# A layer's second expert product: unsplit weight chunks replaced by split ones, with some low parts made on GpSimd

## The chip, the cores and the metric

The kernel runs on one core of one Trainium2 chip. A core has TensorE (PE in the profile; PEld is its weight load), VectorE (DVE), ScalarE (ACT), GpSimd (POOL), SyncE (SP) and 16 DMA engines. The metric is the device time of one execution in microseconds. The kernel before takes 967.09 us (median of three runs, 965.84 to 968.64).

## The reference

One decoder layer on 256 tokens of width 1024. A mixer (a retention branch and a block attention branch, gated and merged) is added to the residual stream. Then comes the part that matters here, a product-key lookup among 16384 single-neuron experts:

```python
def peer(h, w_q, sub_keys, u_tab, v_tab):
    ...
    experts = jnp.take_along_axis(cand_i, pos, axis=-1)      # 16 experts for each of 8 heads, per token
    gates = jax.nn.softmax(top_s, axis=-1).astype(h.dtype)
    ...
        u = u_tab[ec]
        a = jax.nn.gelu(jnp.einsum('td,thkd->thk', hc, u), approximate=False)
        return jnp.einsum('thk,thkd->td', gc * a, v_tab[ec])
```

Both tables are 16384 x 1024 in 32-bit floats (64 MB each). The result is 256 x 1024, in 32-bit floats.

## The kernel before

The kernel first computes the mixer and the queries. For most tokens it then reads the experts densely: the first expert product multiplies the whole table u, in 128 chunks of 128 experts, with the tokens, and the result, after its activation and gates, is the matrix W (128 experts x 128 chunks x 176 token columns). For the remaining tokens it gathers rows: GpSimd issues an indirect DMA for each (line 1026, tiles `rows`), and VectorE adds the row, scaled, to a running sum (line 1112, tiles `vacc` and `accx`).

The second expert product is the loop at the end: for every chunk c of the table v, 8 blocks of 128 columns are multiplied with the chunk's 176 columns of W. Eight PSUM banks `o` add up over all chunks.

A chunk of v arrives by one 512 KB DMA on SP's queue, into one of the six slots of `raw_ring`. There are two ways to multiply it:

- Split. ScalarE copies the chunk to `rhi` in the format fp32r (line 148, the high part), and VectorE subtracts that from the chunk and writes `rlo` (line 149, the low part). This is `split_to`, called by `cut_v`. `cut_w` does the same with W for two chunks at once: `cw` holds the high part (ScalarE, line 1234) and the low part (VectorE, line 1235) side by side. A block is then two matmuls: high part of v with 352 columns (line 1294), and low part of v with 176 columns (line 1295).
- Unsplit. For the ten pairs of chunks that `PLAIN` lists, TensorE multiplies the raw chunk with W in 32-bit floats (line 1292), and neither ScalarE nor VectorE touches them.

`rhi` and `rlo` have four buffers each, taken in turn in the order of the calls, and `cw` has two. The schedule is written by hand: instructions stand on each engine's queue in the order of the calls, each queue runs in order, and semaphores between the engines follow from the tiles that they read and write. In iteration c the program asks for chunk c+2's cut, multiplies chunk c, and takes 0.62 steps of the gather.

## Time and profile before

| | |
|---|---|
| median of the runs | 967.09 us |
| the profiled execution | 966.36 us, its span 964.6 us |
| TensorE busy | 956.3 us (99%) |
| VectorE busy | 770.8 us (80%) |
| ScalarE busy | 518.9 us (54%) |
| GpSimd busy | 362.8 us (38%) |
| moved by DMA | 318.30 MB, 330 GB/s on the mean |

The second expert product begins 672.35 us into the span. Rows of a timeline give the start, the duration, the engine, the line, the operation with what it writes and reads, and in brackets the idle time of the engine just before it with what ended it. Rows of stretches give, for each engine, the busy time and the instructions in it, then TensorE's granted share of its clock, the share of the DMA engines and the rate. In the chain of waits, a row gives the start, the duration, the engine, the tile and the line.

### The profile page before, as it was taken

The numbers are of one execution on the slowest core, as the hardware profiler recorded it, in microseconds if no ns is written. First come the engines' busy times: TensorE is split into PE (matmuls) and PEld (weight loads), VectorE is DVE, ScalarE is ACT, GpSimd is POOL, SyncE is SP. The second block draws the span as 40 slices with busy tenths as digits, with TensorE's granted clock in tenths as the row PEclk, the third lists the DMA queues.
The fourth block names the chain that finished last, engine by engine and source line by source line (L and its number), as shares of the span: only waits on it lengthen the run. The fifth ranks groups of instructions, "written<-read, shape, count | busy, mean of one in ns | idle before, by whom it ended". The sixth has DMA issues, their size and how long they took to land.

```text
span 964.6 us, 19141 instructions
## 1 busy us (share of the span) xinstructions
PE 956.3 (99%) x7216; PEld 917.8 (95%) x7216; DVE 770.8 (80%) x1487; ACT 518.9 (54%) x946; POOL 362.8 (38%) x303
## 2 busy tenths in 40 slices
PE   8999999999999999999999999999999999999998
PEld 6887898998999999999999999999999999999997
DVE  6667667777679997999689998844888888988886
ACT  5555555544654445444667776975454444544443
POOL 2421000000204456444455676744444553554520
PEclk9999999999999999999999999999999999999999
DMA  8877889996798999999999999999999999999993
GB/s 297 243 186 228 241 240 270 305 290 187 243 395 330 407 369 344 380 374 389 370 377 336 367 335 371 384 327 365 331 386 388 390 392 365 386 387 385 380 349 111
DMA packets 108042, 318.30 MB, mean 330 GB/s; under 512 B 11276, under 2 KB 21397, under 8 KB 107822
## 3 DMA queue, kind: packets, MB, share of 16 engines
q1 hardware_dynamic: 64524, 184.43, 53.6%
q0 software_dynamic: 32528, 115.54, 32.2%
q10 hardware_dynamic: 10898, 17.11, 5.9%
q8 instruction: 57, 0.93, 0.4%
q14 instruction: 35, 0.29, 0.1%
HBM read 306.47 MB, written 12.09 MB: 330 GB/s over the span
## 4 chain that ended last, share of the span: by engine, by line
PE 96%; DMA 2%; DVE 1%; issue 0%; ACT 0%; POOL 0%; SPq 0%; ACTq 0%; DVEq 0%; POOLq 0%
PE acc L1262 23%; PE side L736 10%; PE acc L1294 8%; PE side L1294 8%; PE acc L231 6%; PE acc L233 6%; PE acc L232 6%; PE acc L1190 4%; PE acc L1295 4%; PE side L1295 4%; PE acc L241 3%; PE acc L240 3%; PE acc L242 3%; PE side L1292 3%; PE acc L1292 2%; DMA raw_ring<-in_peer_u_dram 2%
## 5 line engine op out<-in xcount | busy, mean ns | idle before, releaser
L1026 POOL DMA_INDIRECT rows<-in_peer_u_dram,eg x86 | 108.2, 1259 | 78.5 <-DVE rows L1037 34.6
L1026 POOL DMA_INDIRECT rows<-in_peer_v_dram,eg x54 | 86.9, 1610 | 90.2 <-DVE vacc L1112 66.7
L736 PE MATMUL side<-ident,raw_ring 128*128 128x128 f32 x816 | 107.2, 274 | 0.8 <-DMA raw_ring<-in_peer_u_dram 0.8
L736 PEld LDWEIGHTS side<-ident,raw_ring 128*128 128x128 f32 x816 | 98.7, 190 | 1.2 <-issue 1.2
L1037 DVE SCALAR_TENSOR_TENSOR rows<-rows,h 128x1024 f32<-128x1024 f32 x43 | 53.2, 1247 | 5.5 <-DMA rows<-in_peer_u_dram,eg 5.3
L1112 DVE SCALAR_TENSOR_TENSOR vacc<-rows,av,vacc 128x1024 f32<-128x1024 f32 x43 | 55.0, 1280 | 0.2
L1205 ACT ACTIVATE W<-acc 128x512 f32<-128x512 f32 (+17 forms) x44 | 28.0, 636 | 32.2 <-DVE W L1203 25.9
L1220 POOL TENSOR_TENSOR W<-W,gl 128x256 f32<-128x256 f32 (+16 forms) x29 | 25.0, 861 | 52.6 <-ACT gl L1219 45.7
L1234 ACT ACTIVATE cw<-W 128x352 fp32r<-128x352 f32 x54 | 26.6, 492 | 31.9 <-PE acc L1295 29.6
L1235 DVE TENSOR_TENSOR cw<-W,cw 128x352 fp32r<-128x352 f32 x54 | 28.1, 521 | 18.2 <-ACT cw L1234 17.8
L1150 DVE TENSOR_TENSOR oh_buf<-niota,tT 128x512 f32<-128x512 f32 x44 | 32.5, 738 | 6.6 <-ACT tT L1172 6.6
L579 POOL DMA_DIRECT2D x1d<-xt x1 | 0.7, 657 | 88.2 <-DVE xt L561 88.2
L155 POOL TENSOR_TENSOR gny<-va,minus_half 128x8 f32<-128x8 f32 x2 | 3.3, 1654 | 69.6 <-DVE va L453 69.6
L1156 ACT ACTIVATE oh_buf<-oh_more,tT 128x128 f32<-128x128 bf16 x88 | 29.4, 425 | 0.1
L1156 ACT ACTIVATE oh_more<-oh_more,tT 128x128 f32<-128x128 bf16 x88 | 29.2, 423 | 0.0
L1203 DVE TENSOR_TENSOR W<-acc,W 128x280 f32<-128x280 f32 (+16 forms) x32 | 24.7, 770 | 5.5 <-PE acc L1190 2.8
L1292 PE MATMUL side<-W,raw_ring 128*128 128x176 f32 x160 | 27.4, 314 | 0.0
L1262 PE MATMUL acc<-hTd,raw_ring 128*128 128x128 f32 x224 | 27.3, 275 | 0.0
L1292 PE MATMUL acc<-W,raw_ring 128*128 128x176 f32 x160 | 27.1, 313 | 0.0
L1262 PEld LDWEIGHTS acc<-hTd,raw_ring 128*128 128x128 f32 x224 | 26.1, 192 | 0.0
L1292 PEld LDWEIGHTS acc<-W,raw_ring 128*128 128x128 f32 x160 | 24.7, 190 | 0.0
L1292 PEld LDWEIGHTS side<-W,raw_ring 128*128 128x128 f32 x160 | 24.3, 190 | 0.0
(2623 smaller groups left out, 3446.2 us busy)
## 6 DMA issues: line engine op xcount, KB each, us to landing
raw_ring<-in_peer_v_dram SPq DMA_DIRECT2D x128, 512.0 KB
raw_ring<-in_peer_u_dram SPq DMA_DIRECT2D x102, 512.0 KB
raw_ring<-in_w_in_dram SPq DMA_DIRECT2D x52, 512.0 KB
raw_ring<-in_peer_w_q_dram SPq DMA_DIRECT2D x16, 512.0 KB
raw_ring<-turned SPq DMA_DIRECT2D x14, 512.0 KB
W<-in_peer_u_dram SPq DMA_DIRECT2D x12, 512.0 KB
raw_ring<-in_ret_w_branch_dram SPq DMA_DIRECT2D x8, 512.0 KB
raw_ring<-in_w_out_dram SPq DMA_DIRECT2D x8, 512.0 KB
```

Source lines behind the costliest of these rows:

```text
L231: T.matmul(o[t], xh[:, s], wh, start=(k == 0), stop=False)
L232: T.matmul(o[t], xh[:, s], wl, start=False, stop=False)
L233: T.matmul(o[t], xl[:, s], wh, start=False, stop=(k == kc - 1))
L736: T.transpose(p[:, k * P:(k + 1) * P], r.rearrange("p (i k) -> p k i", k=KC)[:, 4 * q + k], ident)
L1026: G.indirect_dma_start(out=r, out_offset=None, in_=tab, in_offset=bass.IndirectOffsetOnAxis(ap=eg[:, j:j + 1], axis=0))
L1037: V.scalar_tensor_tensor(r, r, 1.0, h, op0=OP.mult, op1=OP.mult, accum_out=av[:, j:j + 1])
L1112: V.scalar_tensor_tensor(a, r, av[:, j:j + 1], a, op0=OP.mult, op1=OP.add)
L1156: A.activation(o1[:, j], o1b[:, :, j], AF.Copy, scale=tT[:, t, 1, k + j:k + j + 1])
L1262: T.matmul(pa[:, n:n + NA], uT[:, k * P:(k + 1) * P], hT[:, k], start=(c % 2 == 0 and k == 0), stop=(k == KC - 1), skip_group_check=True)
L1292: T.matmul(o[b][:, :ND], vh[:, n], w, start=False, stop=False, skip_group_check=True)
L1294: T.matmul(o[b][:, :2 * ND], vh[:, n], w, start=(c == 0), stop=False, skip_group_check=True)
L1295: T.matmul(o[b][:, :ND], vl[:, n], w[:, :ND], start=False, stop=(c == NK - 1), skip_group_check=True)
```

## The change

All chunks are split, so `PLAIN` and the unsplit branch are gone. Every sixth chunk from 9 on (`LOW_G`: 9, 15, ... 123, twenty chunks) has its low part made by GpSimd, and its cut is asked for in iteration c-3, ahead of the cut of the chunk before it. All others are cut two ahead as before.

```diff
-PLAIN = [4 + 6 * i for i in range(10)]
+LOW_G = range(9, 125, 6)
...
     def cut_v(c):
         if c < NK:
             hi, lo = hi_tile(), lo_tile()
-            split_to(hi, lo, v_raw.pop(c))
+            split_to(hi, lo, v_raw.pop(c), G if c in LOW_G else V)
             v_cut[c] = (hi, lo)
...
     def block(b, c):
         vh, vl, w = cuts[c]
         n = slice(b * P, (b + 1) * P)
-        if vl is None:
-            T.matmul(o[b][:, :ND], vh[:, n], w, start=False, stop=False, skip_group_check=True)
-            return
         T.matmul(o[b][:, :2 * ND], vh[:, n], w, start=(c == 0), stop=False, skip_group_check=True)
         T.matmul(o[b][:, :ND], vl[:, n], w[:, :ND], start=False, stop=(c == NK - 1), skip_group_check=True)
...
     for c in range(NK):
         load_to(len(pieces) + NK + c + 2)
-        if (c + 2) // 2 not in PLAIN:
+        if c + 3 in LOW_G:
+            cut_v(c + 3)
+        if c + 2 not in LOW_G:
             cut_v(c + 2)
-            if c % 2 == 0:
-                cut_w(c + 2)
-        if c // 2 in PLAIN:
-            cuts[c] = (v_raw.pop(c), None, W[:, c, :])
-        else:
-            cuts[c] = (*v_cut.pop(c), w_cut[c - c % 2][:, c % 2])
+        if c % 2 == 0:
+            cut_w(c + 2)
+        cuts[c] = (*v_cut.pop(c), w_cut[c - c % 2][:, c % 2])
```

How the queues change is shown at three places. The first is ScalarE's queue before, around the unsplit chunks 8 and 9 (`rhi__7439` is chunk 7's high part, `rhi__7500` chunk 10's):

```order
L1234 ACTIVATE cw<-W 128x2x176
L148 ACTIVATE rhi__7439<-raw_ring 128x1024
L148 ACTIVATE rhi__7500<-raw_ring 128x1024
L1234 ACTIVATE cw<-W 128x2x176
L148 ACTIVATE rhi__7515<-raw_ring 128x1024
```

and the same place after the change (`rhi__7460` is chunk 9's high part, `rhi__7464` chunk 8's, `rhi__7510` chunk 10's):

```order
+L148 ACTIVATE rhi__7460<-raw_ring 128x1024
+L148 ACTIVATE rhi__7464<-raw_ring 128x1024
+L1234 ACTIVATE cw<-W 128x2x176
+L148 ACTIVATE rhi__7510<-raw_ring 128x1024
+L1234 ACTIVATE cw<-W 128x2x176
+L148 ACTIVATE rhi__7533<-raw_ring 128x1024
```

Chunks 8 and 9 now have high parts and a `cw` of their own, and chunk 9's high part stands ahead of chunk 8's.

The second is VectorE's queue after the change, from chunk 7's low part (`rlo__7440`) over chunk 8's (`rlo__7465`) to chunk 11's (`rlo__7534`):

```order
L149 TENSOR_TENSOR rlo__7440<-raw_ring,rhi__7439 128x1024
L149 TENSOR_TENSOR rlo__7465<-raw_ring,rhi__7464 128x1024
L1235 TENSOR_TENSOR cw<-W,cw 128x2x176
L1112 SCALAR_TENSOR_TENSOR accx<-rows__7172,av,accx 128x1024
L1112 SCALAR_TENSOR_TENSOR accx<-rows__7175,av,accx 128x1024
L149 TENSOR_TENSOR rlo__7511<-raw_ring,rhi__7510 128x1024
L1235 TENSOR_TENSOR cw<-W,cw 128x2x176
L149 TENSOR_TENSOR rlo__7534<-raw_ring,rhi__7533 128x1024
```

Before, chunk 10's low part followed on chunk 7's with only the two gathered rows between. Now chunk 8's low part and its `cw` stand there too; chunk 9's low part isn't on this queue.

The third is GpSimd's queue, before:

```order
L1220 TENSOR_TENSOR W<-W,gl 128x2x128 x4
L1026 DMA rows<-in_peer_v_dram,eg 128x1024 x4
L1026 DMA rows__7496<-in_peer_v_dram,eg 128x1024
L1026 DMA rows__7527<-in_peer_v_dram,eg 128x1024
L1026 DMA rows<-in_peer_v_dram,eg 128x1024 x4
```

and after:

```order
L1220 TENSOR_TENSOR W<-W,gl 128x2x128 x4
L1026 DMA rows<-in_peer_v_dram,eg 128x1024 x3
L149 TENSOR_TENSOR rlo__7461<-raw_ring,rhi__7460 128x1024
L1026 DMA rows<-in_peer_v_dram,eg 128x1024
L1026 DMA rows__7506<-in_peer_v_dram,eg 128x1024
L1026 DMA rows__7553<-in_peer_v_dram,eg 128x1024
L1026 DMA rows<-in_peer_v_dram,eg 128x1024
L149 TENSOR_TENSOR rlo__7605<-raw_ring,rhi__7604 128x1024
```

The gathers are the same ones; after every three to five of them stands the low part of a chunk, here of chunks 9 and 15.

## The prediction

> **What bounds the kernel now.** I read the page's busy table and chain first, then the stretches of the second expert product.

> ```profile
> span 964.6 us, 19141 instructions
> PE 956.3 (99%) x7216; PEld 917.8 (95%) x7216; DVE 770.8 (80%) x1487; ACT 518.9 (54%) x946; POOL 362.8 (38%) x303
> PE 96%; DMA 2%; DVE 1%; issue 0%; ACT 0%; POOL 0%; SPq 0%; ACTq 0%; DVEq 0%; POOLq 0%
> ```

> TensorE is the chain almost from end to end, so time is won by less work on it or lost by a new wait in front of it. The unsplit pairs begin at 690.0, 716.6, 743.2 and so on. Cutting there gives periods of twelve chunks: one unsplit pair and five split pairs.

> ```profile
> core 0: us, PE busy (x) PEld busy (x) DVE busy (x) ACT busy (x) POOL busy (x), PEclk, DMA share, GB/s
> 716.60:743.20 26.60, 26.60 (x194) 26.60 (x194) 22.54 (x23) 12.77 (x15) 10.70 (x7) 1.00 1.00 385
> ...
> 902.70:929.30 26.60, 26.60 (x194) 26.60 (x194) 23.55 (x23) 12.56 (x16) 10.44 (x8) 1.00 1.00 377
> sum 239.30, PE 239.30 PEld 239.30 DVE 205.26 ACT 114.35 POOL 111.35; mean PE 26.59 PEld 26.59 DVE 22.81 ACT 12.71 POOL 12.37
> ```

> Nine periods take 239.3 us, 26.59 each, and TensorE is never idle in them. VectorE works 205.26 / 9 = 22.81 us a period: 3.78 us to spare. ScalarE and GpSimd have half their time free; the DMA engines have almost none.

> **TensorE's gain.** These are the first matmuls of two split chunks eight apart, and two rows of the chain where unsplit pairs begin:

> ```profile
> 723.38 0.35 PE L1294 MATMUL side<-cw,rhi__7778 128*128 128x352 f32 x1
> 740.82 0.36 PE L1294 MATMUL side<-cw,rhi__7961 128*128 128x352 f32 x1
> 716.59 1.22 PE side L1292 x8
> 743.16 1.22 PE side L1292 x8
> ```

> A split chunk takes (740.82 - 723.38) / 8 = 2.18 us, so twelve take 26.16. The old period is 743.16 - 716.59 = 26.57, or 26.59 by the mean of nine. Each of ten periods gains 0.43 us: **-4.3 us** if everything else keeps up.

> **What VectorE must do.** Its work back to back, in one place:

> ```profile
> 718.79 1.22 DVE L149 TENSOR_TENSOR rlo__7779<-raw_ring,rhi__7778 128x1024 fp32r<-128x1024 f32 x1
> 719.93 1.22 DVE L149 TENSOR_TENSOR rlo__7792<-raw_ring,rhi__7791 128x1024 fp32r<-128x1024 f32 x1
> 721.06 0.52 DVE L1235 TENSOR_TENSOR cw<-W,cw 128x352 fp32r<-128x352 f32 x1
> 721.50 1.28 DVE L1112 SCALAR_TENSOR_TENSOR vacc<-rows,av,vacc 128x1024 f32<-128x1024 f32 x1
> 722.69 1.22 DVE L149 TENSOR_TENSOR rlo__7818<-raw_ring,rhi__7817 128x1024 fp32r<-128x1024 f32 x1
> ```

> From start to start, a low part costs 1.14 us, a low part of the weights (`cw`) 0.44, a gathered row's sum 1.19. A period after the change has twelve low parts, of which GpSimd makes two, so VectorE still makes ten. It gets a sixth `cw`: 22.81 + 0.44 = 23.25 us. By that count alone it fits into 26.16.

> **The price of the twenty low parts on GpSimd.** No subtraction of 1024 columns runs there now. The nearest rows are sums and products of two operands; the last VectorE row is the one that they meet.

> ```profile
> 643.99 0.72 POOL L1220 TENSOR_TENSOR W<-W,gl 128x256 f32<-128x256 f32 x1 [3.80 <-ACT gl L1219]
> 66.23 1.28 POOL L325 TENSOR_TENSOR ra<-ra,rb__607 128x512 f32<-128x512 f32 x1 [21.44 <-DVE rb__607 L323]
> 67.48 2.27 POOL L325 TENSOR_TENSOR ra<-ra,rb__613 128x512 f32<-128x512 f32 x1
> 67.36 1.23 DVE L149 TENSOR_TENSOR rlo__624<-raw_ring,rhi__623 128x1024 fp32r<-128x1024 f32 x1
> 68.52 2.32 DVE L149 TENSOR_TENSOR rlo__657<-raw_ring,rhi__656 128x1024 fp32r<-128x1024 f32 x1
> ```

> Undisturbed, 256 columns take 0.72 us and 512 take 1.28; by that slope 1024 take 2.40, an estimate. GpSimd has 14 us free in a period, so two of these fit.

> But the two engines shut each other out. GpSimd's second sum begins at 67.48, just after VectorE began a subtraction (67.36 to 68.59), and lasts 2.27 us: it ends 1.28 after VectorE is through, its whole undisturbed time. VectorE's next subtraction, of the same kind as those in question, begins at 68.52 and takes 2.32 instead of 1.23: it ends 1.08 after GpSimd has ended at 69.75. VectorE lost 1.09 us to 512 columns. A shorter pair agrees:

> ```profile
> 669.64 1.49 POOL L1220 TENSOR_TENSOR W<-W,gl 128x256 f32<-128x256 f32 x1 [3.27 <-ACT gl L1219]
> 669.33 1.22 DVE L149 TENSOR_TENSOR rlo__7279<-raw_ring,rhi__7278 128x1024 fp32r<-128x1024 f32 x1 [0.42 <-ACT rhi__7278 L148]
> 670.55 1.68 DVE L149 TENSOR_TENSOR rlo__7296<-raw_ring,rhi__7295 128x1024 fp32r<-128x1024 f32 x1
> ```

> Here 256 columns cost VectorE 0.46 us and GpSimd 0.77. The same slope takes VectorE's loss to 1.09 + 1.12 = 2.21 us for 1024 columns. All three kinds of VectorE work in this stage read two operands from SBUF, as the delayed subtractions do, so I let all of them be shut out. The bounds are 0 (GpSimd always in a gap of VectorE) and 2.40 (its whole time). I take 2.21, nearest to the same operation's row. The low part taken off VectorE saves 1.14 and costs it 2.21.

> [...] With the whole 2.40 locked a period would be 28.05 instead of 27.67 us and the end result 3.8 us later.

> **The sum.** VectorE's period becomes 23.25 + 2 x 2.21 = 27.67 us, more than TensorE's 26.16 and more than the old 26.59. It becomes the bound and TensorE waits for low parts. Ten periods (chunks 6 to 126) add 10 x (27.67 - 26.59) = 10.8; TensorE's gain is already in this, since it waits.

> VectorE enters with a head start that is used up first. Its first low part ends at 669.33 + 1.22 = 670.55, and TensorE wants that chunk here:

> ```profile
> 672.35 0.41 PE L1294 MATMUL side<-cw,rhi__7278 128*128 128x352 f32 x1
> ```

> That is -1.8 us. Of VectorE's 3.78 us of idleness a period nearly nothing should remain, since its waits are on high parts that are then ready. All of it remaining would be +37.8, none is 0. I take about +1 in all, towards none because a late VectorE finds its inputs waiting. So 10.8 - 1.8 + 1 = **+10.0**.

> **Parts that I cost at nothing.** Twenty more high parts (1.06 us) and ten `cw` copies (0.49) are 2.6 us a period on ScalarE, which has 13.9 free there. The bytes loaded are the same; a raw slot comes free when its low part is made, and no longer after TensorE has read it. At 27.67 us a period the DMA engines need 385 x 26.6 / 27.67 = 370 GB/s. If VectorE did not bind they would need 391, and the split stretch of another period showed 398. GpSimd's gathers queue behind each new subtraction, by up to 2.4 plus 1.2 us of waiting for VectorE. Six rows are in flight and a sum comes every 2.18 / 0.62 = 3.5 us, so about 17 us of lead covers it; without that cover VectorE would wait up to 3.6 us at each of twenty places.

> ```profile
> 827.70:849.50 21.80, 21.80 (x163) 21.80 (x161) 19.08 (x19) 9.60 (x11) 12.99 (x7) 1.00 1.02 398
> 724.03 1.06 ACT L148 ACTIVATE rhi__7838<-raw_ring 128x1024 fp32r<-128x1024 f32 x1 [2.29 <-DMA raw_ring<-in_peer_v_dram]
> 729.92 0.35 PE L1294 MATMUL side<-cw,rhi__7838 128*128 128x352 f32 x1
> ```

> The profiled execution took 966.36 us for its span of 964.6. It becomes 976.4, and the median of the runs shown (967.09) is 0.73 above it: **977 us**.

> **Rivals.**

> *TensorE keeps the pace.* If a GpSimd low part costs VectorE at most (26.16 - 23.25) / 2 = 1.45 us, the ten gains come whole: 967.1 - 4.3 = 962.8. For it: GpSimd starts once ScalarE has written chunk c+3, and ScalarE then spends 1.06 us on chunk c+2, for which VectorE may be idle anyway, so part of the lock could fall into that gap. Against it: with 27.67 us asked of 26.16 there are no gaps left. Chance 0.17.

> *A draw.* At a loss of (26.59 - 23.25) / 2 = 1.67 us the period is the old one, and between 1.6 and 1.8 the time stays within 0.3% (about what a measurement here can tell from no change), at 964 to 970. A larger head start would also lead here. Chance 0.10.

> *ScalarE's new order holds up the chunk ahead.* ScalarE takes chunk c+3 before c+2 at twenty places, and c+3 lands later. In the rows last shown a chunk landed at about 724.0 and was wanted at 729.92, 5.9 us later; the one in front of it 2.18 earlier, 3.7 us after the landing. From the landing of c+3 the new order needs 1.06 (its high part), 2.21 (GpSimd, over the other high part), 1.14 and 0.44: 4.85 us. That is 1.1 late. At half of the places it adds 11 us to the forecast (988), at all 22 (999). It decides once loads land less than 7.0 us ahead of their use. Against it: the ring refills faster without raw chunks held by TensorE, and a slower TensorE lets loads get ahead. Chance 0.13.

> *The forecast*, VectorE bound at 970 to 985: 0.60.

> **Numbers.** The likeliest case gives 977, its own range 970 to 985. Taking in the first rival and the lower half of the third, the range is 962.5 to 989. Faster 0.17, same 0.10, slower 0.73.

> **What would show it.** GpSimd's L149 rows should last 2.4 to 3.6 us, and VectorE rows next to them should grow by about 2.2. VectorE should be busy some 98% between 700 and 930, and TensorE should show idle time ahead of L1294 or L1295 put down to VectorE's `rlo` or `cw`, twenty times 0.7 us on average, with periods of 27.7 us. If TensorE shows no idle time and periods of 26.2, the price of the lock is wrong. If TensorE waits for ScalarE's `rhi`, or ScalarE for DMA at the new places, the third rival holds.

## The result and the profile after

The changed kernel takes 977.47 us (median of six runs, 975.16 to 979.01); the kernel before takes 968.05 beside it (965.84 to 968.64). The ratio is 1.0098, with a 95% interval from 1.0084 to 1.0113: 9.4 us slower. The profiled execution took 977.47 us itself, with a span of 975.7.

The busy table and the shares of the chain, from the page of the changed kernel:

```profile
span 975.7 us, 19251 instructions
PE 957.6 (98%) x7216; PEld 916.8 (94%) x7216; DVE 803.5 (82%) x1497; ACT 543.1 (56%) x976; POOL 431.2 (44%) x323
PE 94%; issue 2%; DVE 2%; POOL 1%; ACT 0%; DMA 0%; ACTq 0%; DVEq 0%; POOLq 0%
```

TensorE's share of the chain falls from 96% to 94%, VectorE's rises from 1% to 2% and GpSimd's from 0% to 1%. How long the stage lasts is read from two rows of its timeline, the first matmul of chunk 0 and that of chunk 126. Line 1291 is now the high part's matmul, line 1292 the low part's (1294 and 1295 before). The third row is the kernel before, its first matmul of chunk 126.

```profile
671.00 0.41 PE L1291 MATMUL side<-cw,rhi__7278 128*128 128x352 f32 x1
964.17 0.35 PE L1291 MATMUL side<-cw,rhi__10277 128*128 128x352 f32 x1
953.07 0.35 PE L1294 MATMUL side<-cw,rhi__10017 128*128 128x352 f32 x1
```

That is 293.2 us for 126 chunks. Before it was 953.07 - 672.35 = 280.7. The stage is 12.4 us longer; the part ahead of it ended 1.35 us earlier in this execution. Against 126 x 2.18 = 274.7 us the excess is 18.5: 12.4 of it are chunks late by over 0.2 us after a wait, 3.4 are two stretches at half clock (below), 1.7 are the small matmuls of the gathered sum near chunk 124, which every version has, and 1.0 is in smaller delays. Before, the excess was 6.0: the same 1.7 and 4.3 for the unsplit pairs.

The waits of TensorE in this stage (what it waited for; us in total, times, longest):

```profile
PE side L1291 <- DVE cw L1235: 7.5, 9, 2.6
PE side L1292 <- DVE rlo__10018 L149: 1.9, 1, 1.9
PE side L1292 <- POOL rlo__8752 L149: 1.1, 1, 1.1
```

The waits sum to 10.5 us. A chunk is late by up to 0.2 us more than its wait, which makes up the rest of the 12.4. TensorE had none of these waits before. Its releaser is VectorE ten times out of eleven, and nine of them name `cw`. Two of the nine periods of twelve chunks, and the sum of all nine:

```profile
core 0: us, PE busy (x) PEld busy (x) DVE busy (x) ACT busy (x) POOL busy (x), PEclk, DMA share, GB/s
711.20:737.30 26.10, 26.10 (x194) 26.10 (x193) 24.02 (x24) 16.00 (x19) 20.05 (x11) 1.00 1.01 384
820.40:851.30 30.90, 28.18 (x194) 27.76 (x193) 26.53 (x24) 15.07 (x19) 18.69 (x11) 0.94 0.96 375
sum 248.30, PE 239.75 PEld 237.40 DVE 233.75 ACT 136.12 POOL 175.74; mean PE 26.64 PEld 26.38 DVE 25.97 ACT 15.12 POOL 19.53
```

The mean period is 248.3 / 9 = 27.59 us, close to the forecast's 27.67. But it isn't made as the forecast had it: periods lie between 26.1 and 30.9 us, and VectorE is busy 233.75 / 248.3 = 94% of the time, not 98%.

Next, the lock itself, at the first place where TensorE is late. The rows are GpSimd's low part of chunk 15, VectorE's work around it, and TensorE's first matmul of chunk 14:

```profile
696.67 2.99 POOL L149 TENSOR_TENSOR rlo__7605<-raw_ring,rhi__7604 128x1024 fp32r<-128x1024 f32 x1
696.19 1.22 DVE L149 TENSOR_TENSOR rlo__7581<-raw_ring,rhi__7580 128x1024 fp32r<-128x1024 f32 x1
697.32 3.42 DVE L1112 SCALAR_TENSOR_TENSOR accx<-rows,av,accx 128x1024 f32<-128x1024 f32 x1
700.67 1.21 DVE L149 TENSOR_TENSOR rlo__7609<-raw_ring,rhi__7608 128x1024 fp32r<-128x1024 f32 x1
701.81 0.51 DVE L1235 TENSOR_TENSOR cw<-W,cw 128x352 fp32r<-128x352 f32 x1
702.37 0.43 PE L1291 MATMUL side<-cw,rhi__7608 128*128 128x352 f32 x1 [0.63 <-DVE cw L1235]
```

GpSimd ends at 699.66, 2.25 us after VectorE's low part is through (697.41). Undisturbed it takes 2.38 (the next place shows it), so it got hardly anything done beside that low part. VectorE's gathered row, 1.28 us undisturbed, takes 3.42: it ends 1.08 after GpSimd, as in the two meetings that the forecast rested on. It lost 2.14 us. Queued behind it are the low part of chunk 14 and its `cw`; the first matmul of chunk 14 waits 0.63 us for them and comes at 702.37, 0.79 us late.

The worst place, chunk 74. ScalarE, GpSimd, VectorE and TensorE in order of time:

```profile
835.83 1.06 ACT L148 ACTIVATE rhi__9036<-raw_ring 128x1024 fp32r<-128x1024 f32 x1 [4.65 <-DMA raw_ring<-in_peer_v_dram]
836.80 1.04 ACT L148 ACTIVATE rhi__9040<-raw_ring 128x1024 fp32r<-128x1024 f32 x1
837.03 2.38 POOL L149 TENSOR_TENSOR rlo__9037<-raw_ring,rhi__9036 128x1024 fp32r<-128x1024 f32 x1 [4.94 <-ACT rhi__9036 L148]
837.87 2.62 DVE L149 TENSOR_TENSOR rlo__9041<-raw_ring,rhi__9040 128x1024 fp32r<-128x1024 f32 x1 [3.83 <-ACT rhi__9040 L148]
840.41 0.51 DVE L1235 TENSOR_TENSOR cw<-W,cw 128x352 fp32r<-128x352 f32 x1
840.98 0.43 PE L1291 MATMUL side<-cw,rhi__9040 128*128 128x352 f32 x1 [2.56 <-DVE cw L1235]
```

Here ScalarE waits 4.65 us for the load of chunk 75 (`rhi__9036`), the one that it now takes ahead of chunk 74 (`rhi__9040`). GpSimd starts as soon as chunk 75's high part is there, just ahead of the low part of chunk 74 on VectorE, which takes 2.62 us instead of 1.21. VectorE had been idle for 3.83 us before it. So VectorE is late at this place though it had time, and TensorE stands still for 2.56 us.

And what follows on it, by stretches of 3.41 us (columns as above; PEclk is the granted clock):

```profile
838.78:842.19 3.41, 1.21 (x9) 1.22 (x10) 3.41 (x4) 2.11 (x3) 2.38 (x2) 1.00 0.51 161
842.19:845.60 3.41, 3.41 (x16) 3.41 (x15) 3.41 (x4) 1.06 (x1) 2.13 (x2) 0.50 0.99 384
845.60:849.00 3.40, 3.40 (x27) 3.40 (x26) 3.40 (x5) 1.45 (x2) 2.75 (x2) 1.00 0.99 387
```

After the stretch in which TensorE worked for only 1.21 us, the clock is 0.50 for exactly one more: 16 matmuls instead of 27, a further 1.7 us. The same happens at 937.77. GpSimd's twenty subtractions last 2.38 to 4.20 us, 3.09 on average; the rows of VectorE beside them are longer than undisturbed ones by 32 us in all, 1.6 us for each subtraction.

### The profile page after: what moved, and what is told of

It is laid out like the page before. It is cut to its first block, busy times and chain, and to the rows that moved or that the text cites. A ratio compares the mean times of both kernels' runs of the same rounds, so it can differ in the third digit from the quotient of the medians.

```text
span 975.7 us, 19251 instructions
## 1 busy us (share of the span) xinstructions
PE 957.6 (98%) x7216; PEld 916.8 (94%) x7216; DVE 803.5 (82%) x1497; ACT 543.1 (56%) x976; POOL 431.2 (44%) x323
## 4 chain that ended last, share of the span: by engine, by line
PE 94%; issue 2%; DVE 2%; POOL 1%; ACT 0%; DMA 0%; ACTq 0%; DVEq 0%; POOLq 0%
PE acc L1262 23%; PE side L736 10%; PE side L1291 9%; PE acc L1291 9%; PE acc L231 6%; PE acc L232 5%; PE acc L233 5%; PE acc L1190 4%; PE side L1292 4%; PE acc L1292 4%; PE acc L241 3%; PE acc L240 3%; PE acc L242 3%; PE side L633 1%; DVE vacc L1112 1%
## 5 line engine op out<-in xcount | busy, mean ns | idle before, releaser
L1026 POOL DMA_INDIRECT rows<-in_peer_u_dram,eg x86 | 105.3, 1225 | 78.0 <-DVE rows L1037 34.9
L1026 POOL DMA_INDIRECT rows<-in_peer_v_dram,eg x54 | 91.2, 1689 | 46.3 <-DVE vacc L1112 26.2
L1112 DVE SCALAR_TENSOR_TENSOR vacc<-rows,av,vacc 128x1024 f32<-128x1024 f32 x43 | 61.2, 1422 | 0.1
L1234 ACT ACTIVATE cw<-W 128x352 fp32r<-128x352 f32 x64 | 31.6, 493 | 52.4 <-PE acc L1292 52.4
L1220 POOL TENSOR_TENSOR W<-W,gl 128x256 f32<-128x256 f32 (+16 forms) x29 | 26.2, 902 | 51.9 <-ACT gl L1219 45.5
L1235 DVE TENSOR_TENSOR cw<-W,cw 128x352 fp32r<-128x352 f32 x64 | 32.8, 513 | 9.8 <-ACT cw L1234 9.8
L1262 PEld LDWEIGHTS acc<-hTd,raw_ring 128*128 128x128 f32 x224 | 26.1, 192 | 0.0
L1112 DVE SCALAR_TENSOR_TENSOR accx<-rows,av,accx 128x1024 f32<-128x1024 f32 x9 | 13.6, 1515 | 12.5 <-DMA rows<-in_peer_v_dram,eg 12.5
L1190 PE MATMUL acc<-oh_buf 128*128 128x128 f32 x176 | 23.4, 276 | 0.0
L1190 PE MATMUL acc<-oh_more,oh_buf 128*128 128x128 f32 x176 | 23.2, 275 | 0.0
L1190 PEld LDWEIGHTS acc<-oh_buf 128*128 128x128 f32 x176 | 21.6, 192 | 0.0
```

The source lines that it names most:

```text
L1026: G.indirect_dma_start(out=r, out_offset=None, in_=tab, in_offset=bass.IndirectOffsetOnAxis(ap=eg[:, j:j + 1], axis=0))
L1112: V.scalar_tensor_tensor(a, r, av[:, j:j + 1], a, op0=OP.mult, op1=OP.add)
L1190: T.matmul(p[:, j * P:(j + 1) * P], o2, o1, start=True, stop=True)
L1262: T.matmul(pa[:, n:n + NA], uT[:, k * P:(k + 1) * P], hT[:, k], start=(c % 2 == 0 and k == 0), stop=(k == KC - 1), skip_group_check=True)
```

## The experiments

Two theories are to be told apart. By the forecast's, VectorE runs out of time because each of GpSimd's subtractions locks it out (**lock**), and the sum over a period decides (**capacity**). By the rival, the new order, with chunk c+3 ahead of c+2, is what makes a chunk late (**order**).

**All low parts on VectorE.** This is the change without GpSimd, in the plain order.

```diff
-LOW_G = range(9, 125, 6)
+LOW_G = ()
```

> All 128 chunks split, every low part made by VectorE, two chunks ahead and in order; GpSimd makes none. The lock theory (a GpSimd low part shuts VectorE out for some 2.2 us and that is what TensorE waits for): VectorE has 22.81 + 0.44 + 2 x 1.14 = 25.5 us of work in a TensorE period of 26.16, so nearly all of the 4.3 us is won: 963 to 967 us. The capacity theory in its strict form (VectorE needs slack for its waits on ScalarE and DMA): TensorE waits again, 967 to 973. The order theory (ScalarE's taking chunk c+3 first is what costs): also 963 to 967, so this run does not tell it from the lock.

Measured: 963.0 us beside 967.49, ratio 0.9956 (0.9938 to 0.9973). TensorE has no wait in the stage. The sum of its nine periods:

```profile
sum 235.50, PE 235.50 PEld 235.50 DVE 228.67 ACT 136.68 POOL 144.01; mean PE 26.17 PEld 26.17 DVE 25.41 ACT 15.19 POOL 16.00
```

The split chunks give the 26.17 us a period that the forecast had (26.16), and VectorE does all twelve low parts in 25.41, 97% of it, without a stall. The simplest form of the change is thus 4.5 us faster than the kernel before, and what GpSimd was to take over need not be taken over at all.

**Plain order, twenty on GpSimd.** Only the order is undone.

```diff
-        if c + 3 in LOW_G:
-            cut_v(c + 3)
         if c + 2 not in LOW_G:
             cut_v(c + 2)
         if c % 2 == 0:
             cut_w(c + 2)
+        if c + 3 in LOW_G:
+            cut_v(c + 3)
```

> As the changed kernel, GpSimd makes the same twenty low parts, but ScalarE takes chunk c+2 and its weights first and chunk c+3 behind them, in the same iteration. Lock theory: VectorE is shut out as before, only at another place in its queue; 972 to 979 us. Order theory: the stalls at chunk c+2 go; 963 to 968 us.

Measured: 971.56 beside 967.49, ratio 1.0042 (1.0028 to 1.0055). Its nine periods, its waits, and the lock at chunk 15 again:

```profile
sum 242.90, PE 237.94 PEld 235.88 DVE 239.66 ACT 136.88 POOL 171.70; mean PE 26.44 PEld 26.21 DVE 26.63 ACT 15.21 POOL 19.08
```

```profile
PE side L1291 <- DVE cw L1235: 3.5, 6, 1.0
PE side L1292 <- POOL rlo__8758 L149: 1.9, 1, 1.9
```

```profile
699.85 1.21 DVE L149 TENSOR_TENSOR rlo__7605<-raw_ring,rhi__7604 128x1024 fp32r<-128x1024 f32 x1
700.98 2.71 DVE L1235 TENSOR_TENSOR cw<-W,cw 128x352 fp32r<-128x352 f32 x1
700.33 2.98 POOL L149 TENSOR_TENSOR rlo__7611<-raw_ring,rhi__7610 128x1024 fp32r<-128x1024 f32 x1 [2.36 <-ACT rhi__7610 L148]
```

This is the forecast's mechanism in its pure form. VectorE is busy 239.66 / 242.90 = 99% of the time, periods take 26.99 us, and each lock costs VectorE 2.0 us (39.3 us over twenty; here 2.2 on a `cw`). Chunk 14's low part has begun before GpSimd starts and keeps its 1.21 us, and only its `cw` is held up. The chunks lose 8.5 us beside the small matmuls of every version, where the changed kernel lost 16.8 (12.4 in gaps, 3.4 at half clock, 1.0 in smaller gaps).

**The changed kernel's order, GpSimd without the lock.** GpSimd writes zeros instead of the difference: the low parts of v of twenty chunks are left out of the product.

```diff
-            split_to(hi, lo, v_raw.pop(c), G if c in LOW_G else V)
+            src = v_raw.pop(c)
+            if c in LOW_G:
+                A.activation(hi, src, AF.Copy)
+                G.memset(lo.bitcast(F32), 0.0)
+            else:
+                split_to(hi, lo, src)
```

> As the changed kernel with ScalarE's order kept, but in place of the twenty subtractions GpSimd writes zeros into the low part, which reads nothing (the low parts of these twenty chunks of v are left out of the result). Lock theory: VectorE's rows beside GpSimd's keep 1.2 to 1.3 us, the stalls of TensorE go, 963 to 966 us. Order theory: the stalls at chunk c+2 stay, 972 to 979 us.

Measured: 962.6 beside 967.49, ratio 0.9943 (0.993 to 0.9957), and no wait of TensorE in the stage. Its nine periods and the place of chunk 15:

```profile
sum 235.45, PE 235.45 PEld 235.45 DVE 207.94 ACT 136.46 POOL 124.63; mean PE 26.16 PEld 26.16 DVE 23.11 ACT 15.16 POOL 13.85
```

```profile
698.09 0.97 POOL L1230 MEMSET rlo__7605<- 128x1024 f32 x1
697.63 1.22 DVE L149 TENSOR_TENSOR rlo__7581<-raw_ring,rhi__7580 128x1024 fp32r<-128x1024 f32 x1
698.77 1.27 DVE L1112 SCALAR_TENSOR_TENSOR accx<-rows,av,accx 128x1024 f32<-128x1024 f32 x1
```

VectorE's rows beside it keep their 1.22 and 1.27 us, and its own work is 23.11 us a period (23.25 in the forecast). Without the subtraction nothing is left of the loss: 977.5 - 962.6 = 14.9 us hang on it. Other things change with it, though: the zeros are sooner written than the difference (0.97 us against 2.38), they don't wait for the high part, and the raw slot comes free without GpSimd having read it.

**The order alone.** The order of the changed kernel, with VectorE making those low parts. It leaves nothing out of the product, and VectorE reads the raw slot and waits for the high part as GpSimd did, so it answers those objections as far as the order goes.

```diff
-            split_to(hi, lo, v_raw.pop(c), G if c in LOW_G else V)
+            split_to(hi, lo, v_raw.pop(c))
```

> As the changed kernel with its order (every sixth chunk cut three ahead, ahead of the chunk before it), but VectorE makes these low parts too, so that no lock is there and VectorE is as full as with all low parts on it. If the new order costs only through the lock behind it: 962 to 965 us, as with all low parts on VectorE in plain order. If the order costs by itself once VectorE is full: 966 to 970 us.

Measured: 962.72 beside 967.08, ratio 0.9956 (0.994 to 0.9973), no wait of TensorE in the stage. The order by itself costs nothing against the 963.0 of the plain one.

**Half as many.** Plain order, ten low parts on GpSimd.

```diff
-LOW_G = range(9, 125, 6)
+LOW_G = range(9, 125, 12)
```

(with the order edit of the second experiment)

> Plain order (chunk c+2 and its weights first), ten low parts on GpSimd in place of twenty (every twelfth chunk); VectorE makes the other ten. Zero gave 963.0 and twenty 971.6. If VectorE's capacity decides (23.1 us of other work, 1.14 for each low part, about 2.0 lost to each lock): 23.1 + 1.14 + 2.0 = 26.2 us in a period of 26.16, just full: 963 to 966 us. If each lock makes its own delay whatever VectorE has to spare: half-way, 967 us.

Measured: 962.88 beside 967.08, ratio 0.9962 (0.9949 to 0.9974), no wait of TensorE in the stage.

```profile
sum 235.44, PE 235.44 PEld 235.44 DVE 230.88 ACT 136.84 POOL 158.16; mean PE 26.16 PEld 26.16 DVE 25.65 ACT 15.20 POOL 17.57
```

VectorE lost 16.4 us to ten locks, 1.6 each, and was busy 25.65 of 26.16 us. As long as the sum fits, the locks are invisible in the time. Nor is anything won: with none on GpSimd VectorE was busy 25.41.

**The subtraction in two halves.** The changed kernel, GpSimd working on 512 columns at a time.

```diff
-            split_to(hi, lo, v_raw.pop(c), G if c in LOW_G else V)
+            src = v_raw.pop(c)
+            if c in LOW_G:
+                A.activation(hi, src, AF.Copy)
+                for n in (slice(0, 512), slice(512, 1024)):
+                    G.tensor_tensor(lo[:, n], src[:, n], hi[:, n].bitcast(F32), op=OP.subtract)
+            else:
+                split_to(hi, lo, src)
```

> As the changed kernel, but each GpSimd subtraction in two halves of 512 columns (1.28 us each undisturbed). Lock theory with VectorE's capacity as the limit: the same 2.2 to 2.6 us are lost at each place, 976 to 980 us. If the length of one lock is what makes a chunk late: VectorE gets an instruction in between, and the stalls shrink, 970 to 975 us. Order theory: no difference, 977.

Measured: 973.67 beside 967.49, ratio 1.006 (1.0039 to 1.0081). VectorE lost about as much, 38.0 us or 1.9 per chunk, but in two pieces. The longest wait of TensorE is 1.25 us instead of 2.56, no stretch of the trace is at half clock, and the chunks lose 11.9 us. The median is 3.8 us below the changed kernel's. That this comes from the length of a single lock is not shown: two later traces of the changed kernel, given below, have no half clock either and lose 11.4 us, no more than this one.

**The lock put into the kernel before.** Twenty subtractions on GpSimd whose result isn't read, with the unsplit pairs kept.

```diff
+LOCK = range(6, 126, 6)
...
+            if c in LOCK:
+                G.tensor_tensor(lo_tile(F32), v_raw[c], v_raw[c], op=OP.subtract)
             split_to(hi, lo, v_raw.pop(c))
```

> The kernel before with its unsplit pairs, plus twenty GpSimd subtractions of 1024 columns (a raw chunk from itself, into a low-part buffer that nothing reads), spread evenly, one every sixth chunk; all results are computed as before. The price of the lock by itself: VectorE's 22.81 us a period become 22.81 + 2 x 2.0 = 26.8 against 26.59, so full or a little over: 968 to 974 us, and VectorE rows beside GpSimd's grow to 2.5 to 3.5 us. If the lock did not matter: 967 us and no longer rows.

Measured: 975.48 beside 967.08, ratio 1.01 (1.0079 to 1.0121). The kernel before becomes slower too, and by more than expected. The profiled execution, the fastest of the four at 971.62, shows the wait on `cw` that the kernel before never had, but also one of VectorE on GpSimd:

```profile
PE side L1297 <- DVE cw L1238: 3.8, 5, 1.4
DVE rlo__9531 L150 <- POOL rlo__9532 L1229: 1.8, 1, 1.8
```

VectorE's rows beside GpSimd's lost 23.1 us (1.16 for each), which its idle time would cover: 22.81 + 2 x 1.16 = 25.1 of 26.59 us a period. But there are seven waits like the second line, in which VectorE stood idle until the added subtraction was through. These are semaphore waits of the program, not stretched rows. TensorE's two longest waits (1.16 and 1.38 us, at 847.94 and 902.85) follow on two of them. The extra operation also takes a buffer out of the rotation of low parts. So this run doesn't price the lock, and how the excess is divided isn't settled.

**The changed kernel again, and the plain order again.** One trace of the changed kernel has two stretches at half clock, and its difference from the plain order was not measured side by side. So it was measured twice more, the second time beside the plain order.

> The changed kernel once more, for a second trace of it: if the halvings of TensorE's clock behind its two longest stalls (2.62 and 2.12 us) belong to the kernel, stalls of over 2 us are followed by about 3.4 us at a clock of 0.5 here too; if they were a chance of one execution, there are none. 975 to 979 us.

> The changed kernel again, beside the same kernel in plain order on one chip. If its order costs beyond the lock: 975 to 979 us, some 5 us over plain order. If the difference seen before lay in the executions (one trace of it had two halvings of TensorE's clock, another none, 977.47 against 972.18 us): 972 to 975, within 2 us of plain order, with a wider spread.

> The changed kernel with ScalarE taking chunk c+2 and its weights ahead of chunk c+3, again: 970.5 to 973 us, as before.

Measured: the changed kernel 972.18 (one run, beside 967.08) and then 977.22 (973.36 to 981.22) beside 967.89, ratio 1.0105 (1.0058 to 1.0153); the plain order 971.47 beside 967.89, ratio 1.0042 (1.0026 to 1.0059). So the order adds 977.2 - 971.5 = 5.7 us, the same as before (977.47 - 971.56 = 5.9, measured apart). The changed kernel's four runs here spread over 8 us, the six of the first measurement over 4. In the profiled executions of the changed kernel at 972.18 and 974.93 us no stretch is at half clock and the chunks lose 11.4 us each time, 2.9 more than the 8.5 in the plain order; in the one at 977.47 they lose 16.8 with the half clock. (The plain order's second trace has one stretch at half clock too. The two long stalls that the first expectation gives as 2.62 and 2.12 us are 2.56 and 1.94 by TensorE's waits.) The waits of the one at 974.93 are more even. These are the first two lines; three more on VectorE's low parts last 1.2, 0.7 and 0.7 us:

```profile
PE side L1291 <- DVE cw L1235: 4.0, 9, 0.7
PE side L1292 <- DVE rlo__10018 L149: 1.5, 1, 1.5
```

Where do the 5.7 us lie? In the traces the stage, from chunk 0 to chunk 126, takes 293.2, 287.8 and 287.8 us in the changed kernel, and 284.9 and 285.7 in the plain order: 4.3 apart on the mean. The half clock is only a part of that. A stretch of 3.41 us at half clock lowers the mean granted clock of an execution by 0.0017. Over the ten runs of the changed kernel in the two larger measurements that clock is 0.9978, over the twenty of the plain order 0.9985: a difference of 0.0007 x 977 = 0.7 us of 5.7. The rest are gaps as far as the traces show it. Single executions also differ ahead of the stage, where the two kernels are alike: chunk 0 begins at 671.1 us in the one of 972.18 us and at 673.9 in the one of 974.93, and this is the whole difference between these two.

**What halves the clock.** The kernel before, with two to seven added subtractions on VectorE ahead of the low part of nine chunks, so that TensorE stalls for different times.

```diff
+LATE = dict(zip(range(18, 126, 12), (2, 3, 3, 4, 4, 5, 5, 6, 7)))
...
+            if c in LATE:
+                x = lo_tile(F32)
+                for _ in range(LATE[c]):
+                    V.tensor_tensor(x, v_raw[c], v_raw[c], op=OP.subtract)
             split_to(hi, lo, v_raw.pop(c))
```

> The kernel before, with 2, 3, 3, 4, 4, 5, 5, 6 and 7 extra subtractions of 1.2 us on VectorE ahead of the low part of chunk 18, 30, ... 114 (into a buffer that nothing reads), so that TensorE stalls for 0 to some 7 us at nine places. If a stall that fills over half of a clock window of 3.41 us halves the clock for the next one: every stall over 3.4 us is followed by 3.4 us at 0.5, stalls of 2 to 3.4 us are followed by it only where most of the stall lies in one window (windows counted from the halvings), those under 1.7 us never. If only stalls longer than a whole window do it: none under 3.4 us is followed by it.

Measured: 1017.36 us, with stalls of 2.66, 1.48, 1.71, 1.98, 4.21, 6.15, 3.51, 5.93 and 5.90 us. Half clock followed on all but the one of 1.48. Three pairs of stretches, the one with the stall and the one behind it:

```profile
742.26:745.67 3.41, 1.93 (x15) 1.72 (x14) 3.41 (x5) 1.06 (x1) 0.12 (x1) 1.00 0.97 377
745.67:749.08 3.41, 3.41 (x27) 3.41 (x27) 3.08 (x3) 0.30 (x1) 2.77 (x2) 1.00 0.74 250
769.57:772.98 3.41, 1.70 (x13) 1.49 (x12) 3.27 (x5) 1.06 (x1) 0.00 (x0) 1.00 1.04 413
772.98:776.39 3.41, 3.41 (x15) 3.41 (x14) 3.37 (x4) 1.06 (x1) 1.68 (x1) 0.50 0.81 280
800.29:803.70 3.41, 1.43 (x11) 1.22 (x11) 3.41 (x4) 0.90 (x1) 0.00 (x0) 1.00 1.02 407
803.70:807.11 3.41, 3.41 (x16) 3.41 (x15) 3.37 (x4) 0.16 (x1) 1.52 (x1) 0.50 0.87 274
```

TensorE idle for 1.48 of 3.41 us, 43%: full clock. Idle for 1.71, 50%: half clock for the next stretch. The borders of the stretches are read from the changes of the granted clock in each trace, which lie whole stretches apart (842.19 and 937.77 in the changed kernel: 28 of them). The two traces of the plain order show that the borders matter. Both have a stall of 1.9 us at the same place, for the low part of chunk 63. The first two rows are the first trace, the others the second:

```profile
810.30:813.71 3.41, 2.36 (x17) 2.12 (x16) 3.41 (x4) 2.51 (x3) 3.39 (x2) 1.00 0.90 326
813.71:817.12 3.41, 2.55 (x18) 2.55 (x19) 3.41 (x3) 0.26 (x1) 2.96 (x3) 1.00 0.87 303
812.67:816.08 3.41, 1.51 (x11) 1.45 (x11) 3.41 (x2) 0.88 (x1) 3.27 (x2) 1.00 0.95 334
816.08:819.49 3.41, 3.41 (x15) 3.41 (x15) 3.32 (x4) 1.45 (x2) 2.80 (x3) 0.50 0.93 317
```

In the first the stall falls across a border, 1.05 and 0.86 us in each stretch, and the clock stays whole. In the second all of it falls into one stretch, and the next is at half. So in these traces neither the length of a stall nor its count tells the two apart, but how long TensorE was idle in one stretch: 0.50 followed on 1.71 us of 3.41 (50%) and more, full clock on 1.48 (43%) and less. The whole stretches of the changed kernel and of the kernel before agree: 0.50 followed on 1.94, 2.20 and 3.21 us in the one and on 1.66 (49%, at 958.90) in the other, full clock on the rest, which were idle for 1.29 us at most.

After the stalls of 3.5 us and more, two stretches are at half clock. The mean granted clock of the execution, 0.978 over 1015.6 us, is a loss of 22.3 us, or about 13 of these stretches at 1.7 each, which is what one after each of 2.66, 1.71 and 1.98 us and two after each of the other five give. One such pair:

```profile
902.69:906.10 3.41, 2.67 (x11) 2.67 (x11) 3.41 (x5) 1.06 (x1) 1.26 (x1) 0.50 0.53 165
906.10:909.51 3.41, 3.41 (x16) 3.41 (x15) 3.23 (x3) 0.00 (x0) 2.45 (x3) 0.50 0.80 274
```

At half clock, a stretch with 0.74 us idle was followed by another at half; at full clock, one with 1.05 us idle (810.30 above) was followed by one at 1.00.

## Why the prediction came out right, and where not

The time was right, 977.5 for 977.0, and the sign with it. That it agrees to 0.5 us is luck: two errors of about equal size cancel in it.

**TensorE's gain (-4.3 us)** is right. Where VectorE keeps up, a period is 26.16 or 26.17 us, and the kernels are 4.2 to 4.9 us faster than the one beside them.

**VectorE's own work (23.25 us a period)** is right: 23.11 measured with its two low parts gone and no lock.

**GpSimd's undisturbed subtraction (2.40 us)** is right: 2.38.

**The price of the lock (2.21 us)** is the term that was mis-sized. VectorE is shut out as the forecast describes it, and a VectorE instruction that meets it at work loses 2.1 to 2.2 us (2.7 once). But it isn't met at work each time: at places like chunk 74 VectorE was idle until the lock had already run for 0.8 us, and lost 1.4. The mean is 1.6 us in the profiled execution, 1.8 and 2.0 in two others, and 2.0 in the plain order. The first rival had named just this gap, behind ScalarE's work on chunk c+2; it is real but does not come down to the 1.45 us that this rival needed. Why the mean differs between executions was not followed further. One reading behind the term was off: in the meeting at 67.48, GpSimd ended 69.75 - 68.59 = 1.16 us after VectorE was through, not 1.28. GpSimd's own rows, put at 2.4 to 3.6 us, last 2.38 to 4.20.

VectorE's rows grew beside GpSimd's subtraction, which reads two operands, and not beside its writing of zeros, which reads none: a low part of 1.21 us took 2.62 beside the one (chunk 74), and 1.22 and 1.27 stayed beside the other. All three kinds of VectorE work were held up by the subtraction, as the forecast let them be: besides the low part a gathered row took 3.42 us for 1.28, and a `cw` 2.71 for 0.51 (plain order).

**VectorE's remaining idleness (+1 in all)** failed: it is 248.30 - 233.75 = 14.6 us in nine periods. This is how the two errors meet: a period is 25.97 us of work and 1.62 of idleness, where the forecast had 27.67 and 0.1.

**The sum by capacity (+10.0)** was thus right only as a number. With 2.0 us a lock the period needs 23.11 + 4.0 = 27.1 us; ten of them cost some 5 us more than before, less the head start of 1.8: about +3.4. That is the plain order, measured at +4.1 and +3.6, with VectorE at 99%. At ten locks the same sum gives 23.11 + 1.14 + 1.6 = 25.9 us of 26.16 and no loss, as measured.

**The order of ScalarE's work** was given only as a rival (0.13), with 11 us or more on top. It is worth 5.7 us and was missing from the forecast's sum. Its mechanism is half of the rival's: ScalarE does wait for c+3's load with c+2 behind it, but that alone hurts nothing (962.72 with the order and no GpSimd). It takes the order and the lock together: with neither the kernel takes 963.0 us, with the order alone 962.7, with the lock alone 971.5, with both 977.3. GpSimd's start is tied to the high part of c+3, which puts the lock ahead of chunk c+2's low part and `cw`, the two that TensorE wants next. Of the changed kernel's eleven waits all but two are at the chunk just ahead of one of GpSimd's; the two are at chunk 115, two ahead of one, and at chunk 63, which is GpSimd's own. In the plain order chunk c+2's low part comes first.

**"Twenty stalls of 0.7 us"** failed likewise: there are about eleven, of 0.2 to 2.6 us, in periods of 26.1 to 30.9. **VectorE at 98%** failed as a sign in the changed kernel (94%).

**At nothing:** ScalarE's extra work and GpSimd's gathers were rightly put at nothing: versions with the same ScalarE work have no stall, and VectorE's longest waits in the changed kernel (3.8 and 2.4 us) are all for ScalarE's high parts, none for a gathered row. The loads are not nothing under the new order, since a late one now holds two chunks (4.65 us at 835.83). And the clock was left out: two stretches at half speed are 3.4 us of the profiled execution; over the runs it is about 0.7 us more than in the plain order.

Unsettled are the excess of the kernel before with subtractions added, whether two halves in place of one subtraction help by themselves, and what makes up the slower runs of the changed kernel: its profiled executions lost 11.4 us twice and 16.8 once, and its other runs have no trace.

The simplest version, all chunks split and every low part on VectorE, takes 963.0 us and is faster than both kernels. No version measured is clearly better. Ten low parts on GpSimd (962.9) are no better than none.

## What to carry to other kernels

Before work goes to a helper engine, compare what it saves the busy engine with what the meeting costs it: here 1.14 us saved against 1.6 to 2.0 lost, so each hand-over made VectorE busier. Try first whether the busy engine can do it all: 97% busy without a stall was fast enough, and two opposite errors in a sum that comes out right are found only by undoing one part at a time. Where an operation that locks others must stay, don't let it start just ahead of the work wanted soonest: here that made 5.7 us.

## What the runs showed of the hardware

GpSimd's writing of 1024 columns took 0.97 us and left VectorE's rows at 1.22 and 1.27 us, where its subtraction of as many took 2.38 undisturbed and made VectorE's rows beside it longer by 1.6 us on the mean: in these runs it was the operation that reads that cost something.
